# FFN norm factor on the products' results, a first pair of inner tiles without block sums, and weights transferred ahead of operands

## The chip, the cores and the metric

The kernel runs on one core of a Trainium2 chip. The metric is device time in microseconds (us) of one execution; lower is better. TensorE (PE in the profile) multiplies, VectorE (DVE), ScalarE (ACT) and GpSimd (POOL) work elementwise, and SyncE (SP) issues the transfers between the chip's memory (DRAM) and the on-chip buffers. Results of matmuls stand in eight banks of PSUM.

## What is computed

One step of a decoder layer for 1024 prompt tokens and eight decode tokens, all in float32; the kernel treats the 1032 tokens together. Cut to what the change touches:

```python
def rmsnorm(x, g):
    xf = x.astype(jnp.float32)
    y = xf * lax.rsqrt(jnp.mean(xf * xf, axis=-1, keepdims=True) + EPS)
    return (y * g.astype(jnp.float32)).astype(x.dtype)

def swiglu_half(x, g, w_gate, w_up, w_down):
    u = rmsnorm(x, g)
    return x + 0.5 * ((jax.nn.silu(u @ w_gate) * (u @ w_up)) @ w_down)

def hybrid_layer(x, p_emb, pos, lp, attend, retain):
    h = swiglu_half(x, lp['ffn1_norm'], lp['ffn1_w_gate'], lp['ffn1_w_up'], lp['ffn1_w_down'])
    u = rmsnorm(h, lp['mix_norm'])
    z = u @ lp['w_in']
    ...
    merged = (jax.nn.sigmoid(ga) * (o_att @ lp['w_branch_att'])
              + jax.nn.sigmoid(gr) * (o_ret @ lp['w_branch_ret']))
    h = h + merged @ lp['w_out']
    h = swiglu_half(h, lp['ffn2_norm'], lp['ffn2_w_gate'], lp['ffn2_w_up'], lp['ffn2_w_down'])
    gate = jax.nn.sigmoid(rmsnorm(h, lp['ple_norm']) @ lp['w_ple_gate'])
    ...
```

D_MODEL is 1024 and D_FF 2816. The norm's factor, the rsqrt of the mean square, is one number per token; the gain `g` is one number per feature.

## The kernel before

**Layout.** Features lie on the 128 partitions, tokens on the free axis: a token tile `ht` has 8 row tiles (`k`) of 128 features. The 1032 tokens are two halves (`tp` 0 and 1) of two columns each (`lr`), HC = 258 tokens a column. Every operand of a product is split into a high and a low part (`split`: ACT's cast at L103, then DVE's subtraction at L104), and each product is three matmuls, high·high, high·low, low·high.

**FFN, gate and up** (`Block.run`). The 22 inner tiles of 128 are taken in 11 pairs. For one pair, `unit` forms the 2×2 block product (two inner tiles by two halves of the features, against two halves of the features by two columns) from seven block products instead of eight: 7 × 4 × 3 = 84 matmuls per token half, at L323, L325 and L326. That needs sums of weight blocks (`Stream.early` and `Stream.make`, L264, L265, L281, L285) and sums of token blocks. The latter are made once per FFN by the generator `tokens(tp)`: squares (L437, L438), the norm factor `r` by Newton steps (`rstd2`, L340 to L359), `ht` times gain times `r` (`normed`, L456), sums (L465 to L480), and the splits into the seven blocks `b`. Both FFNs begin with units of pair 0 for `tp` 0 alone, while `tokens(1)` runs beside them; pair 0 for `tp` 1 is done at the end, between the two halves of pair 10. Results go through `gate` (ACT's Silu) and `up` into `s`, and from there to DRAM as `mid_d`.

**FFN, down** (`product`, L369 to L371). All 22 `m` tiles of a token half are loaded back (`fetch`, L600), and for each half `tp` and each half `o` of the features 22 weights are run into eight banks, 24 matmuls a weight. `Rows` transfers the weights (`wd`, L306), with three loads ahead. The evacuation at L618 is one operation a bank: 0.5 times the bank plus `h`.

**w_out** is the same `product`, with four banks, 64 weights of 256 columns and 12 matmuls a weight. Its operands `wm` are the merged branches that the stage before has stored to `mg_d` (L1310) and that are loaded at L1323, eight for each token half; `ht` is loaded at L1325. Evacuation (L1338), squares and, for `tp` 0, the token blocks of FFN 2 run beside it.

**What sets the order.** The program is written through a framework that orders the instructions of each engine by itself from the dependences and the pools' free buffers; each engine then runs its list in order. SP issues all of the transfers above in one list, so a transfer that waits holds up those behind it.

Of the kernel before, what the change touches and what calls it, by code (L numbers as in the profile page):

```python
# [10 lines left out]
F32 = mybir.dt.float32  # L11
# [9 lines left out]
P = 128  # L21
D = 1024
# [34 lines left out]
def body(ctx, tc, a):  # L57
# [240 lines left out]
    class Rows(Stream):  # L298


        def make(self, units):
            raws = []
            for i in range(len(units) + 3):
                if i < len(units):
                    t = self.rawp.tile([P, 512], F32, tag="q", name="wd")[:, :units[i].shape[-1]]
                    sp.dma_start(t, units[i])  # L306
                    raws.append(t)
                if i >= 3:
                    yield self.split(raws[i - 3])
# [66 lines left out]
    class Next:  # L376
# [5 lines left out]
        def open(self, prepare):  # L382
# [3 lines left out]
            self.first = prepare(self.ring)  # L386
# [23 lines left out]
    class Block:  # L410
# [5 lines left out]
        def open(self):  # L416
            self.w_st, self.right = ExitStack(), ExitStack()
            self.x0_st = ExitStack()
            pre = self.pre
            self.wp = self.w_st.enter_context(pools(pre + "w", 6))  # L420
            self.rawp = self.w_st.enter_context(pools(pre + "q", 8))
            bp = self.right.enter_context(pools(pre + "b0", side="right"))
            self.x1 = self.right.enter_context(pools(pre + "x1", side="right"))
            x0 = self.x0_st.enter_context(pools(pre + "x0", side="right"))
            self.bs = [bp.tile([P, 4, 7, 2, HC], F32R, name="b0"), None]
            self.hts = [x.tile([P, KT, 2 * HC], F32, name="ht") for x in (x0, self.x1)]

        def accs(self):
            return [self.x1.tile([P, HC], F32, tag=f"acc{i}", name="acc") for i in range(2)]

        def sq(self, accs, k, hv):
            for i in range(2):
                if k == 0:
                    act.activation(accs[i], hv[:, HV[i]], AF.Square)
                else:
                    t = self.x1.tile([P, HC], F32, tag="sq", name="sq", bufs=4)
# [3 lines left out]
        def tokens(self, tp, accs=None):  # L440

            ht, gi = self.hts[tp], self.gi
            if accs is None:
                accs = self.accs()
                for k in range(KT):
                    self.sq(accs, k, ht[:, k])
                    if k % 2:
                        yield
            r = [self.x1.tile([P, HC], F32, tag=f"r{i}", name="r") for i in range(2)]
            yield from rstd2(accs, D, r)  # L450
            bt = self.bs[tp]
            b11, b12, b21, b22 = (ht[:, 4 * i:4 * i + 4, HV[lr]] for i in range(2) for lr in range(2))

            def normed(t, half, lr):
                for k in range(4):
                    dve.scalar_tensor_tensor(t[:, k], t[:, k], gain(gi, 4 * half + k), r[lr], op0=ALU.mult, op1=ALU.mult)  # L456

            def splits(q, t):
                split(bt[:, :, q, 0], bt[:, :, q, 1], t)

            normed(b11, 0, 0)
            splits(0, b11)
            yield
            normed(b12, 0, 1)
            dve.tensor_tensor(b11, b12, b11, op=ALU.subtract)  # L465
            splits(1, b11)
            yield
            normed(b22, 1, 1)
            dve.tensor_tensor(b11, b22, b11, op=ALU.subtract)
            splits(2, b11)  # L470
            yield
            normed(b21, 1, 0)
            splits(3, b21)
            yield
            dve.tensor_tensor(b12, b22, b12, op=ALU.subtract)
            splits(4, b12)
            yield
            splits(6, b22)
            yield
            dve.tensor_tensor(b11, b21, b11, op=ALU.subtract)  # L480
            splits(5, b11)
            yield

        def stream(self):
# [4 lines left out]
        def run(self, builds, nxt, nxt_st, prepare):  # L489

            pre, bs, NP = self.pre, self.bs, NF // 2
            e_st = ExitStack()
            e = e_st.enter_context(pools(pre + "e", 18))
            stream = self.weights
# [1066 lines left out]
```

## Time and profile before

| quantity | value |
| --- | --- |
| runs, us | 2611.8, 2610.56, 2608.18 (median 2610.56) |
| profiled execution: its own time, its span | 2606.3 us, 2604.5 us |
| TensorE busy | 2455.9 us, 94% of the span |
| VectorE, ScalarE, GpSimd busy | 55%, 37%, 7% |
| mean granted clock of TensorE | 0.974 |
| moved | 355.24 MB, 136 GB/s over the span |

A group's row has line, engine, operation, output <- inputs, shapes and count, then busy us and the mean ns of one, then the idle time of the engine just before them and what ended it. A row of waits has engine, tile and line, what it waited for, and us in total, times, longest. A row of windows has busy us and instruction count of each engine, the granted clock of TensorE as a share of full speed, the busy share of the transfer engines, and GB/s.

### The profile page before, as it was taken

The numbers are of one execution on the slowest core, as the hardware profiler recorded it, in microseconds if no ns is written. First come the engines' busy times: TensorE is split into PE (matmuls) and PEld (weight loads), VectorE is DVE, ScalarE is ACT, GpSimd is POOL, SyncE is SP. The second block draws the span as 40 slices with busy tenths as digits, with TensorE's granted clock in tenths as the row PEclk, the third lists the DMA queues.
The fourth block names the chain that finished last, engine by engine and source line by source line (L and its number), as shares of the span: only waits on it lengthen the run. The fifth ranks groups of instructions, "written<-read, shape, count | busy, mean of one in ns | idle before, by whom it ended". The sixth has DMA issues, their size and how long they took to land.

```text
span 2604.5 us, 48647 instructions
## 1 busy us (share of the span) xinstructions
PE 2455.9 (94%) x19036; PEld 2364.9 (91%) x19036; DVE 1435.4 (55%) x3271; ACT 962.4 (37%) x2125; POOL 175.5 (7%) x220
## 2 busy tenths in 40 slices
PE   5999999899999999999999974979999998999998
PEld 5899999899999999999976664979999998999997
DVE  8765657733333656422577763696656676332345
ACT  5444445523222112211255531454444454222221
POOL 0000000001011101100142100000000000010111
PEclk9899999899999999999999987999999998999999
DMA  3223323869422122222034369333323248684311
GB/s 131 98 82 121 120 85 128 299 255 327 150 100 73 62 68 72 88 75 89 31 102 125 100 198 325 119 104 110 119 86 115 99 144 326 241 308 134 128 52 66
DMA packets 177031, 355.24 MB, mean 136 GB/s; under 512 B 19433, under 2 KB 68738, under 8 KB 176802
## 3 DMA queue, kind: packets, MB, share of 16 engines
q1 hardware_dynamic: 171682, 338.54, 37.8%
q0 software_dynamic: 5120, 13.59, 1.5%
q8 instruction: 150, 2.46, 0.4%
q14 instruction: 79, 0.65, 0.1%
HBM read 259.21 MB, written 91.80 MB: 135 GB/s over the span
## 4 chain that ended last, share of the span: by engine, by line
PE 87%; DVE 6%; DMA 4%; ACT 1%; issue 1%; POOL 0%; SPq 0%; DVEq 0%; POOLq 0%; ACTq 0%
PE ps L325 11%; PE ps L323 11%; PE ps L326 11%; PE ps L369 8%; PE ps L371 7%; PE ps L370 7%; PE ps L138 7%; PE ps L139 7%; PE ps L140 7%; PE ps L1074 2%; PE ps L1110 1%; PE ps L1099 1%; DVE w L104 1%; DMA wm<-mg_d 1%; DVE b L104 1%
## 5 line engine op out<-in xcount | busy, mean ns | idle before, releaser
L323 PE MATMUL ps<-b,w 128*128 128x258 f32 x2464 | 703.6, 286 | 10.9 <-ACT b L103 9.5
L325 PE MATMUL ps<-b,w 128*128 128x258 f32 x2464 | 706.9, 287 | 5.0 <-DVE b L104 5.0
L326 PE MATMUL ps<-b,w 128*128 128x258 f32 x2464 | 697.1, 283 | 12.3 <-DVE w L104 12.3
L326 PEld LDWEIGHTS ps<-b,w 128*128 128x128 f32 x2464 | 474.6, 193 | 12.9 <-DVE w L104 12.9
L323 PEld LDWEIGHTS ps<-b,w 128*128 128x128 f32 x2464 | 468.8, 190 | 13.7 <-ACT b L103 11.3
L325 PEld LDWEIGHTS ps<-b,w 128*128 128x128 f32 x2464 | 472.4, 192 | 6.6 <-DVE b L104 6.6
L369 PE MATMUL ps<-m,w 128*128 128x258 f32 x1408 | 401.8, 285 | 23.8 <-DMA m<-mid_d 23.8
L370 PE MATMUL ps<-m,w 128*128 128x258 f32 x1408 | 399.2, 284 | 0.0
L371 PE MATMUL ps<-m,w 128*128 128x258 f32 x1408 | 398.5, 283 | 0.0
L104 DVE TENSOR_TENSOR w<-wd,w 128x512 fp32r<-128x512 f32 (+1 forms) x240 | 152.8, 646 | 372.1 <-ACT w L103 347.7
L138 PE MATMUL ps<-u,w 128*128 128x344 f32 (+4 forms) x960 | 312.0, 326 | 3.8 <-DVE sz L147 3.8
L104 DVE TENSOR_TENSOR w<-wq,w 128x512 fp32r<-128x512 f32 x312 | 213.7, 688 | 180.5 <-ACT w L103 178.3
L139 PE MATMUL ps<-u,w 128*128 128x344 f32 (+4 forms) x960 | 308.5, 321 | 0.0
L140 PE MATMUL ps<-u,w 128*128 128x344 f32 (+4 forms) x960 | 307.9, 321 | 0.0
L369 PEld LDWEIGHTS ps<-m,w 128*128 128x128 f32 x1408 | 267.9, 190 | 24.2 <-DMA m<-mid_d 24.2
L103 ACT CAST w<-wd 128x512 fp32r<-128x512 f32 (+1 forms) x240 | 134.5, 561 | 416.1 <-PE ps L371 307.2
L370 PEld LDWEIGHTS ps<-m,w 128*128 128x128 f32 x1408 | 269.2, 191 | 0.0
L371 PEld LDWEIGHTS ps<-m,w 128*128 128x128 f32 x1408 | 268.0, 191 | 0.0
L103 ACT CAST w<-wq 128x512 fp32r<-128x512 f32 x312 | 191.9, 621 | 58.0 <-PE ps L326 34.2
L138 PEld LDWEIGHTS ps<-u,w 128*128 128x128 f32 (+1 forms) x960 | 180.5, 188 | 6.2 <-DVE sz L147 3.8
L139 PEld LDWEIGHTS ps<-u,w 128*128 128x128 f32 (+1 forms) x960 | 180.0, 187 | 0.9 <-issue 0.4
L140 PEld LDWEIGHTS ps<-u,w 128*128 128x128 f32 (+1 forms) x960 | 180.1, 188 | 0.6
(297 smaller groups left out, 3706.3 us busy)
## 6 DMA issues: line engine op xcount, KB each, us to landing
mid_d<-s SPq DMA_DIRECT2D x88, 516.0 KB, 3.7
m<-mid_d SPq DMA_DIRECT2D x88, 516.0 KB, 6.0
wd<-in_f1down_dram SPq DMA_DIRECT2D x88, 256.0 KB, 3.7
wd<-in_f2down_dram SPq DMA_DIRECT2D x88, 256.0 KB, 4.1
ct<-in_cache_dram SPq DMA_DIRECT2D x128, 128.0 KB, 2.1
wq<-in_f1gate_dram SPq DMA_DIRECT2D x52, 256.0 KB, 4.1
wq<-in_f1up_dram SPq DMA_DIRECT2D x52, 256.0 KB, 2.6
wq<-in_f2gate_dram SPq DMA_DIRECT2D x52, 256.0 KB, 4.1
```

Of the source, the lines that this page charges most:

```text
L103: act.copy(dst_hi, src)
L104: dve.tensor_tensor(dst_lo, src, dst_hi.bitcast(F32), op=ALU.subtract)
L138: pe.matmul(ps, w[:, 0, ws], x[:, 0, xs], start=start, stop=False)
L139: pe.matmul(ps, w[:, 0, ws], x[:, 1, xs], start=False, stop=False)
L140: pe.matmul(ps, w[:, 1, ws], x[:, 0, xs], start=False, stop=stop)
L323: pe.matmul(ps, w[:, 0, js], t[:, 0], start=q in (0, 1, 3) and j == 0, stop=False, skip_group_check=True)
L325: pe.matmul(ps, w[:, 0, js], t[:, 1], start=False, stop=False, skip_group_check=True)
L326: pe.matmul(ps, w[:, 1, js], t[:, 0], start=False, stop=j == kh - 1, skip_group_check=True)
L369: pe.matmul(ps, w[:, 0, ws], t[:, 0, HV[n % 2]], start=f == 0, stop=False)
L370: pe.matmul(ps, w[:, 0, ws], t[:, 1, HV[n % 2]], start=False, stop=False)
L371: pe.matmul(ps, w[:, 1, ws], t[:, 0, HV[n % 2]], start=False, stop=f == nf - 1)
L1074: pe.matmul(ps[:, :w], qc[hd][:, i * P:(i + 1) * P], kc[hd][:, j:j + w], start=True, stop=not diag)
```

## The change

- The norm factor leaves the token blocks. `plain_tokens` scales `ht` by the gain alone (DVE for `tp` 0, ACT for `tp` 1); `r` is kept in a pool of its own and multiplied into the gate results before Silu, and, with the 0.5, into the down results. The up results are not scaled.
- The first pair of inner tiles is done with eight block products (`plain`), on blocks that need no sums, for (tile, half) (0,0), (1,0), (1,1), (0,1), with 12 weights from `Rows`. `sums` and `last_sum` make the other blocks meanwhile. An FFN then has 384 matmuls in place of 336 for this pair, and `stream` starts with pair 1. At the end pair 10 is done for `tp` 0, then for `tp` 1.
- `Rows` issues its first three transfers when it is made, which in `w_out` and in the down product is ahead of the operands. In `w_out` only the operands of `tp` 0 are fetched first; those of `tp` 1 after the first product; `ht` after five `wm`.
- Ring loads for the stage after an FFN are issued behind the last `m` load. `mst` has four buffers instead of two. The raw weights' pool is closed after the gate and up units and opened again with five buffers.

```diff
     class Rows(Stream):
+        def __init__(self, wp, rawp, units, ahead):
+            super().__init__(wp, rawp, units, ahead)
+            self.units, self.raws = iter(units), []
+            for _ in range(3):
+                self.fetch()
...
+        def plain_tokens(self, tp, k0=0, k1=KT):
+
+            ht = self.hts[tp]
+            b11, b12, b21, b22 = self.blocks(tp)
+            for i, (qs, ts) in enumerate((((0, 1), (b11, b12)), ((3, 6), (b21, b22)))):
+                for k in range(4 * i, 4 * i + 4):
+                    if tp == 0:
+                        dve.tensor_scalar(ht[:, k], ht[:, k], gain(self.gi, k), None, op0=ALU.mult)
+                    else:
+                        act.activation(ht[:, k], ht[:, k], AF.Copy, scale=gain(self.gi, k))
+                    yield
+                for q, t in zip(qs, ts):
+                    self.splits(tp, q, t)
+                    yield
...
-            self.weights = Stream(self.wp, self.rawp, [u_ for p_ in pair for u_ in p_] + pair[0] + pair[-1], 0)
+            self.weights = Stream(self.wp, self.rawp, [u_ for p_ in pair[1:] for u_ in p_] + pair[-1], 2)
...
+            def plain(ws, tp, lr):
+                ps = allbank()
+                for h_ in range(2):
+                    for j in range(4):
+                        js, t = slice(j * P, j * P + P), bs[tp][:, j, (0, 1, 3, 6)[2 * h_ + lr]]
+                        pe.matmul(ps[:, :HC], ws[h_][:, 0, js], t[:, 0], start=h_ + j == 0, stop=False)
+                        pe.matmul(ps[:, :HC], ws[h_][:, 0, js], t[:, 1], start=False, stop=False)
+                        pe.matmul(ps[:, :HC], ws[h_][:, 1, js], t[:, 0], start=False, stop=h_ + j == 4)
+                return ps
...
+            for n, (l, tp) in enumerate(((0, 0), (1, 0), (1, 1), (0, 1))):
+                if n != 2:
+                    ws = [rows.take() for _ in range(4)]
+                pg = [plain(ws[:2], tp, lr) for lr in range(2)]
+                if n in (0, 2) and accs[tp] is not None:
+                    for _ in self.norm(tp, accs[tp]):
+                        pass
+                pu = [plain(ws[2:], tp, lr) for lr in range(2)]
+                ts = []
+                for lr in range(2):
+                    t = pt()
+                    ts.append(t)
+                    dve.tensor_tensor(t, pg[lr][:, :HC], self.r[tp][:, HV[lr]], op=ALU.mult)
+                    act.activation(t, t, AF.Silu)
...
             def gate(q, tp, ps):
...
-                elif q == 5:
+                    return
+                r = self.r[tp][:, HV[q in (4, 6)]]
+                if q == 5:
                     gated[tp, q] = t = et()
-                    act.activation(t, ps, AF.Silu)
+                    dve.tensor_tensor(t, ps, r, op=ALU.mult)
+                    defer(1, act.activation, t, t, AF.Silu)
                 else:
                     gated[tp, q] = t = kept[tp, {3: 0, 4: 1, 6: 2}[q]]
                     dve.tensor_tensor(t, t, ps, op=ALU.add)
-                    defer(1, act.activation, t, t, AF.Silu)
+                    defer(1, silu, t, r)
...
-            for i, tp in ((NP - 1, 0), (0, 1), (NP - 1, 1)):
+            for tp in TPS:
                 unit(stream, b, 4, (tp,), gate, tick)
-                unit(stream, b, 4, (tp,), up(i, sgp), tick)
+                unit(stream, b, 4, (tp,), up(NP - 1), tick)
...
+                        if tp == 1 and o == 0:
+                            with tc.issue_after(self.loaded.ins):
+                                nxt.first = prepare(nxt.ring)
...
-                            dve.scalar_tensor_tensor(hv, banks[n][:, :HC], 0.5, hv, op0=ALU.mult, op1=ALU.add)
+                            t = tmp.tile([P, HC], F32, tag="c", name="c")
+                            dve.scalar_tensor_tensor(t, banks[n][:, :HC], 0.5, self.r[tp][:, HV[n % 2]],
+                                                     op0=ALU.mult, op1=ALU.mult)
+                            dve.tensor_tensor(hv, hv, t, op=ALU.add)
...
-                st = mt.tile([P, 2, 2 * HC], F32R, tag="mst", name="mst")
+                st = mt.tile([P, 2, 2 * HC], F32R, tag="mst", name="mst", bufs=4)
...
-        for tp in TPS:
+
+        def fetch(tp):
             for f in range(KT):
                 xs[tp, f] = t = wm.tile([P, 2, 2 * HC], F32R, tag="wm", name="wm")
                 sp.dma_start(t.bitcast(F32), mg_d[f, tp])
-            for k in range(0, KT, 4):
-                sp.dma_start(two.hts[tp][:, k:k + 4], hs_d[:, k:k + 4, both(tp)])
...
+                if f == KT // 2:
+                    for k in range(0, KT, 4):
+                        sp.dma_start(two.hts[tp][:, k:k + 4], hs_d[:, k:k + 4, both(tp)])
+
+        fetch(0)
...
+                if tp == 0 and o == 0:
+                    fetch(1)
...
-                steps = two.tokens(0, accs)
+                steps = chain(two.norm(0, sums_of[0]), two.plain_tokens(0), two.sums(0))
```

How the lists move is seen at three places. First VectorE at the start of FFN 1, from the last squares to the first token blocks (`acc`: sums of squares, `sv`, `sz`, `st`: Newton steps of the norm, `w`: low halves of weights, `b_97`, `b_105`: low halves of token blocks). Before:

```order
L438 TENSOR_TENSOR acc<-acc,sq 128x258 x4
L456 SCALAR_TENSOR_TENSOR ht<-ht,gains,r 128x258 x4
L104 TENSOR_TENSOR w<-wq,w 128x512
L456 SCALAR_TENSOR_TENSOR ht<-ht,gains,r 128x258
L264 TENSOR_TENSOR ws<-wq 128x512
L104 TENSOR_TENSOR b_97<-ht,b_97 128x4x258
L265 TENSOR_TENSOR wq<-wq 128x512
```

And in the changed kernel:

```order
L472 TENSOR_SCALAR ht<-ht,gains 128x516
L104 TENSOR_TENSOR b_105<-ht,b_105 128x4x258
L453 TENSOR_TENSOR acc<-acc,sq 128x258
L104 TENSOR_TENSOR b_105<-ht,b_105 128x4x258
L472 TENSOR_SCALAR ht<-ht,gains 128x516 x3
L350 TENSOR_SCALAR sv<-ps_276 128x6
L453 TENSOR_TENSOR acc<-acc,sq 128x258
```

The first two low halves of token blocks now stand ahead of the norm's Newton steps (`sv` on), where before the first stood behind all of them and behind the scaling at L456.

Second, SP between the last gate and up results of FFN 1 and its down product; in brackets is what an issue waits for (DMAHW: an earlier transfer of SP, by its slot; the other names are engines). Before:

```order
L533 DMA mid_d<-s 128x1032 [waits DMAHW0_49,DVE_49]
L533 DMA mid_d<-s 128x1032 [waits DMAHW1_49,DVE_49]
L608 DMA h<-in_xT_dram 128x4x516 [waits DMAHW2_49]
L600 DMA m<-mid_d 128x1032 [waits DMAHW3_49,DMAHW1_49]
L600 DMA m<-mid_d 128x1032 [waits DMAHW4_49]
```

And in the changed kernel:

```order
L514 DMA mid_d<-s 128x1032 [waits DVE_49] x2
L673 DMA h<-in_xT_dram 128x4x516
L665 DMA m<-mid_d 128x1032 [waits DMAHW4_49]
L665 DMA m<-mid_d 128x1032 [waits DMAHW5_49]
L665 DMA m<-mid_d 128x1032 [waits DMAHW6_49]
```

The first `m` waited for the slot of the last `mid_d` store too (DMAHW1), and now waits for one older transfer only.

Third, SP from the last stores of the merged branches to the weights of `w_out`. Before:

```order
L1310 DMA mg_d<-mst 128x1032
L1325 DMA ht<-hs_d 128x4x516
L1310 DMA mg_d<-mst 128x1032 x2
L1325 DMA ht<-hs_d 128x4x516
L1323 DMA wm<-mg_d 128x1032 x16
L306 DMA wd<-in_wout_dram 128x256 x20
```

And in the changed kernel, where four more `wm` rows stand some 40 issues earlier, among the gate loads of the stage before:

```order
L1383 DMA mg_d<-mst 128x1032 x3
L1397 DMA wm<-mg_d 128x1032 x2
L311 DMA wd<-in_wout_dram 128x256 x3
L1400 DMA ht<-hs_d 128x4x516 x2
L1397 DMA wm<-mg_d 128x1032 x2
L311 DMA wd<-in_wout_dram 128x256 x11
L1397 DMA wm<-mg_d 128x1032 x5
L1400 DMA ht<-hs_d 128x4x516 x2
L1397 DMA wm<-mg_d 128x1032 x3
```

All of `wm` and `ht` stood ahead of the first weight; now two `wm` do, and the second half's operands follow the fourteenth weight.

More of the change, by code (lines that the diff above doesn't have):

```diff
@@ L298, in body, with fetch @@
     class Rows(Stream):
-        def make(self, units):
[L302 to L309, printed above, removed]
+        def __init__(self, wp, rawp, units, ahead):
[3 more added lines that the diff above has]
+                self.fetch()
+        def fetch(self):
+            src = next(self.units, None)
+            if src is not None:
+                t = self.rawp.tile([P, 512], F32, tag="q", name="wd")[:, :src.shape[-1]]
+                sp.dma_start(t, src)
+                self.raws.append(t)
+        def make(self, units):
+            for _ in units:
+                self.fetch()
+                yield self.split(self.raws.pop(0))
     xbank, ybank, zbank = rotation(0, 4), rotation(4, 2), rotation(6, 2)
@@ L435, in sq @@
                 else:
-                    t = self.x1.tile([P, HC], F32, tag="sq", name="sq", bufs=4)
+                    t = self.x1.tile([P, HC], F32, tag="sq", name="sq", bufs=3)
                     act.activation(t, hv[:, HV[i]], AF.Square)
                     dve.tensor_tensor(accs[i], accs[i], t, op=ALU.add)
[L440 to L450, printed above, removed]
-            bt = self.bs[tp]
[L452 to L464, printed above, removed]
-            dve.tensor_tensor(b11, b12, b11, op=ALU.subtract)
[L466 to L473, printed above, removed]
@@ new lines, in norm, with blocks, splits @@
+        def norm(self, tp, accs):
+            return rstd2(accs, D, [self.r[tp][:, HV[lr]] for lr in range(2)])
+        def blocks(self, tp):
+            return [self.hts[tp][:, 4 * i:4 * i + 4, HV[lr]] for i in range(2) for lr in range(2)]
+        def splits(self, tp, q, t):
+            bt = self.bs[tp]
+            split(bt[:, :, q, 0], bt[:, :, q, 1], t)
+        def plain_tokens(self, tp, k0=0, k1=KT):
[11 more added lines that the diff above has]
+                    yield
@@ L474, in tokens, with sums @@
+        def sums(self, tp):
+            b11, b12, b21, b22 = self.blocks(tp)
+            dve.tensor_tensor(b11, b12, b11, op=ALU.subtract)
             yield
             dve.tensor_tensor(b12, b22, b12, op=ALU.subtract)
-            splits(4, b12)
+            self.splits(tp, 4, b12)
             yield
-            splits(6, b22)
+            dve.tensor_tensor(b22, b22, b11, op=ALU.subtract)
+            self.splits(tp, 2, b22)
             yield
-            dve.tensor_tensor(b11, b21, b11, op=ALU.subtract)
@@ L492, in run @@
             e_st = ExitStack()
             e = e_st.enter_context(pools(pre + "e", 18))
-            stream = self.weights
+            stream = self.stream()
             now, due = [0], {}
@@ L525, in gate, with up @@
                     dve.tensor_tensor(t, t, ps, op=ALU.add)
[L526 to L533 removed]
+                    defer(1, silu, t, r)
+            def up(i):
                 def evac(q, tp, ps):
@@ L599, in fetch @@
                 mids[tp, f] = t = mp.tile([P, 2, 2 * HC], F32R, tag="m", name="m")
-                sp.dma_start(t.bitcast(F32), self.mid_d[f, tp])
+                self.loaded = sp.dma_start(t.bitcast(F32), self.mid_d[f, tp])
             for f in range(NF):
@@ L633, in run @@
                             nxt.squares(tmp, tp, 4 * o + k, ht[:, k])
+            self.q_st.close()
             self.w_st.close()
@@ L639, in body @@
     one.open()
-    one.stream().ahead = 1
     for tp in TPS:
@@ L645, in body @@
     mix = Next(ring_st, "r", 1, u1_d)
-    one.run([one.tokens(tp) for tp in TPS], mix, u_st, lambda ring: [ring.load("rv", i) for i in range(2)])
+    one.run(mix, u_st, lambda ring: [ring.load("rv", i) for i in range(2)])
     ring, u, r, wv0 = mix.ring, mix.u, mix.r, mix.first
@@ L1291, in fetch @@
                 gates[tp, o, lr].append(t)
+        for i in range(2):
+            wa[i] = ring.load("batt", i)
         for at in todo[:5]:
@@ L1350, in body @@
     last = Next(ctx, "s", 3, u2_d)
-    two.run([None, two.tokens(1, accs)], last, ctx, lambda ring: [ring.load("plg", o) for o in range(2)])
+    last = Next(ctx, "s", 3, u2_d)
+    two.run(last, ctx, lambda ring: [ring.load("plg", o) for o in range(2)], [None, sums_of[1]])
     ring, u, r, plw = last.ring, last.u, last.r, last.first
```

121 lines of the change are left out of this document (74 added, 47 removed).

## The prediction

> **What bounds the kernel now.** I read the page first: the busy shares, the chain that ended last, the costliest groups.
>
> ```profile
> span 2604.5 us, 48647 instructions
> PE 2455.9 (94%) x19036; PEld 2364.9 (91%) x19036; DVE 1435.4 (55%) x3271; ACT 962.4 (37%) x2125; POOL 175.5 (7%) x220
> PE 87%; DVE 6%; DMA 4%; ACT 1%; issue 1%; POOL 0%; SPq 0%; DVEq 0%; POOLq 0%; ACTq 0%
> L323 PE MATMUL ps<-b,w 128*128 128x258 f32 x2464 | 703.6, 286 | 10.9 <-ACT b L103 9.5
> L326 PE MATMUL ps<-b,w 128*128 128x258 f32 x2464 | 697.1, 283 | 12.3 <-DVE w L104 12.3
> L369 PE MATMUL ps<-m,w 128*128 128x258 f32 x1408 | 401.8, 285 | 23.8 <-DMA m<-mid_d 23.8
> ```
>
> TensorE bounds: 87% of the chain, and only 2604.5 − 2455.9 = 148.6 us in which it has no matmul. So a gain can come only from that idle time, from matmuls run at the slow clock, or from fewer matmuls, and the change adds matmuls. Next, windows, to learn the pace and to see where PE falls short of it.
>
> ```profile
> 200.00:400.00 200.00, 200.00 (x1663) 200.00 (x1662) 121.40 (x247) 91.80 (x208) 0.00 (x0) 1.00 0.29 102
> 25.00:45.00 20.00, 12.90 (x56) 11.50 (x57) 18.27 (x28) 11.01 (x16) 0.00 (x0) 1.00 0.12 40
> 0.00:95.00 95.00, 36.93 (x112) 25.17 (x113) 0.93 0.32 113
> 1700.00:1777.00 77.00, 32.51 (x111) 22.25 (x111) 0.93 0.34 114
> ```
>
> Columns: length, busy time (count) of PE, weight loads, VectorE (DVE), ScalarE (ACT), GpSimd, clock, DMA share, GB/s; the last two rows hold line L323 alone, so PE and weight loads only. The pace is 200/1663 = 0.1203 us a matmul. In 25:45 there are 56, where 166 would fit, and DVE is busy for 18.27 of 20 us. L323 is a third of an FFN's gate/up matmuls: 3 × 112 = 336, one pair of inner tiles for both token halves, is done at 95 us in FFN 1, and 3 × 111 = 333 at 1777 (336 at 1777.5) in FFN 2. I compare the changed kernel at these two points, since what follows them is dense in both.
>
> **First pair of FFN 1.** Waits and matmul starts in 0:120, and VectorE's groups up to 92 us:
>
> ```profile
> PE ps L340 <- DVE acc L438: 11.5, 1, 11.5
> PE ps L323 <- ACT b L103: 9.5, 7, 3.9
> PE ps L325 <- DVE b L104: 5.0, 6, 1.3
> 25.26 0.42 PE L326 MATMUL ps<-b,w 128*128 128x258 f32 x1
> ...
> 27.20 0.42 PE L326 MATMUL ps<-b,w 128*128 128x258 f32 x1
> L104 DVE TENSOR_TENSOR b<-ht,b 128x1032 fp32r<-128x1032 f32 x14 | 16.9, 1230 | 0.7 <-ACT b L103 0.7
> L456 DVE SCALAR_TENSOR_TENSOR ht<-ht,gains,r 128x258 f32<-128x258 f32 x32 | 13.7, 481 | 0.7 <-ACT r L351 0.7
> L104 DVE TENSOR_TENSOR w<-wq,w 128x512 fp32r<-128x512 f32 x19 | 12.7, 683 | 1.5 <-ACT w L103 1.5
> 21.99 0.69 DVE L104 TENSOR_TENSOR w<-wq,w 128x512 fp32r<-128x512 f32 x1 [0.73 <-ACT w L103]
> L1093 DVE TENSOR_SCALAR pr<-pr,rs 128x640 f32<-128x640 f32 x8 | 4.4, 548 | 0.1
> ```
>
> PE starves on token blocks `b`: each needs the norm factor, four L456 and a 1.23 us low half. Between bursts it idles, and inside one the matmuls stand (27.20 − 25.26)/9 = 0.215 us apart (nine steps, unbroken), the slow pace, though the clock of 25:45 reads 1.00. The change takes the factor out of this path: gains only (a 128x516 tensor_scalar, estimated just under the 548 ns of the 640-wide row), and the plain pair reads four blocks that are slices of the scaled tokens, so no sums come first. Blocks and first weights are then ready at about 20.7 us (first low weight at 21.99 before; the squares no longer stand ahead of all of it). The pair takes 384 matmuls instead of 336. From 20.7: 384 × 0.1203 = 46.2, about 2 for the norm's rank-one matmuls, 2.4 for a cold start (priced below), makes 71.3. VectorE has to keep up: 16 block halves × 1.23 = 19.7, 8 sums of the same size 9.8, 17 weight operations of 512 columns × 0.68 = 11.6, 28 accumulations and 24 evacuations of 258 columns × 0.36 = 18.7 (pace from the evacuation row below), 8 scalings × 0.5 = 4, Newton steps about 4: 67.8 us from 5.7 on, so until 73.5. That is a tie with PE; I add 3 and put the end at 74.3. Gain 95 − 74.3 = 20.7, taken as 21. Bounds: 25 if VectorE never delays PE, 10 if each of some ten hand-overs costs the mean L323 wait of 9.5/7.
>
> **w_out and the first pair of FFN 2.** Waits of PE in 1585:1760, SP's issues, and VectorE in w_out:
>
> ```profile
> PE ps L369 <- ACT w L103: 33.0, 2, 32.7
> PE ps L326 <- DVE w L104: 10.0, 2, 9.7
> PE ps L371 <- DVE w L104: 4.4, 4, 1.9
> 1588.39 0.63 SPq L1325 DMA_DIRECT2D ht<-hs_d  x1
> 1589.12 17.68 SPq L1323 DMA_DIRECT2D wm<-mg_d  x16
> 1607.82 12.45 SPq L306 DMA_DIRECT2D wd<-in_wout_dram  x13
> 1590.00:1620.00 30.00, 2.39 (x11) 2.39 (x12) 2.22 (x6) 2.19 (x6) 0.00 (x0) 0.50 0.96 366
> 510.00:515.00 5.00, 3.51 (x16) 3.51 (x17) 0.00 (x0) 0.00 (x0) 0.00 (x0) 0.50 1.00 398
> 515.00:520.00 5.00, 5.00 (x37) 5.00 (x36) 0.69 (x1) 0.68 (x2) 0.00 (x0) 0.81 1.03 420
> L104 DVE TENSOR_TENSOR w<-wd,w 128x256 fp32r<-128x256 f32 x17 | 6.4, 417 | 1.8 <-ACT w L103 1.8
> ```
>
> The largest single wait, 32.7 us, names ScalarE, but it is a weight: the first `wd` is issued at 1607.82 behind 16 `wm` of 0.53 MB and an `ht`, at 366 GB/s. In the new order four `wm` are loaded during the stage before (in place of two `ht`), and only two `wm` and the weights themselves lie between the last store, about 1588.4, and the third weight: 1.06 + 0.39 MB at 366 GB/s is 4 us, 2 to land and cast, so PE restarts at 1595. A cold start: 16 + 37 matmuls in the 8.5 us after 511.5, where 53 × 0.1203 = 6.4 would do, so 2.1, say 2.4 to be safe. The queue then bites back twice. The fourth weight is behind `ht` x2 and `wm` x2, 3.2 MB or 8.6 us, against three cold weights' work of 12 × 3 × 0.215 = 7.7: 1 us. The fifteenth is behind the second half's eight `wm` and two `ht`, 6.3 MB or 17 us, against the six or seven weights then buffered, 12 × 0.1203 = 1.44 each: 7.5 us and a second cold start, 10 in all. w_out has 64 weights × 12 = 768 matmuls: 1595 + 92.4 + 2.4 + 1 + 10 = 1700.8. In the second half VectorE makes 32 halves of weights (417 ns), one set of plain blocks and its sums, about 40 us in 46, so the first FFN units find blocks ready and the 9.7 and the 4.4 us waits go. 384 matmuls (46.2) and 2 for the norm: 1749, with 2.5 of slack 1751.5. Gain 1777.5 − 1751.5 = 26. Bounds: 36 without the queue's stall, 11 if it is twice that and VectorE is 5 late.
>
> **Up to down, in each FFN.** The chain at 501 us and PE's two waits:
>
> ```profile
> 501.45 4.12 DMA mid_d<-s
> 505.58 5.86 DMA m<-mid_d
> PE ps L369 <- DMA m<-mid_d: 11.8, 1, 11.8
> PE ps L369 <- DMA m<-mid_d: 12.0, 1, 12.0
> ```
>
> Here `m` of tile 0 waits for the last store's landing (4.12), and then lands in 5.86 behind an `h` load. In the new order the first four `m` wait only for a queue slot, so they follow at once; store and `h` still pass first, about 2.1 MB. Four ring loads of 0.5 MB that ran there move into the down product. I take 3.5 each, 7 together; bounds 3 (stores late by the last pair) and 12 (the whole 4.12 and the rings' share).
>
> **What it costs.** Evacuating the down banks:
>
> ```profile
> 575.10 2.92 DVE L618 SCALAR_TENSOR_TENSOR h<-ps,h 128x258 f32<-128x258 f32 x8 [1.94 <-PE ps L371]
> PE ps L665 <- DMA u<-u_d: 3.4, 1, 3.4
> PE ps L349 <- DVE sz L147: 2.5, 1, 2.5
> ```
>
> Eight banks in 2.92 us, 0.36 each, are now two operations each, 5.9 us. Between products the banks come free every 0.74 us, while the next product needs one every 3 × 0.1203 = 0.36; but the first evacuation can start 2.5 us before the product ends, so of 8 × 0.74 = 5.9 about 0.3 shows: six such boundaries, 2 (0 to 6). At a block's end 3 us join the norm chain behind the last bank, of which the two waits above are part; `u` loads now stand behind one store instead of three and more matmuls cover the Newton steps: 1.5 per block, 3 (0 to 8). In the units of the last pair, one token half each, VectorE does nearly 20 us in 20.2 us of PE: 1 (0 to 5). In ten pairs per FFN, eight more multiplications per gate unit: 8 × 0.36 = 2.9 us in 40.4 us of PE, on top of 121.40/200 = 61%, so 68%: nothing on the path, since PE is busy through all of 200:400 beside it; if that cover were gone it would be 20 × 2.9 = 58. The third `batt`'s place in the queue is the same; two more `mst` buffers are part of the 26. Pair 0 is no longer taken up again for the second half at the end of an FFN: its matmuls are in the 384, and the 16 raw weights of its two visits become 12, which only eases the queue. The 96 added matmuls (11.5 us) are in both ends above already. Costs 6 (0 to 19).
>
> **Sum.** 21 + 26 + 7 − 6 = 48 off the profiled execution's 2606.3: 2558.3. The median of the runs is 2610.56, 4.3 more; I predict 2562.6, so 2563. All terms at their low ends give 10 + 11 + 3 − 19 = 5, at their high ends 25 + 36 + 12 = 73.
>
> **Rivals.** First, weights still behind operands: the first `ht` of w_out, and the fourth weight behind it, wait for the last three stores to land; if that takes 4 us longer under a full queue, and only two weights are buffered at the second half's loads, the stalls are 4 + (17 − 2 × 1.44 − 7.5) = 10.6 more: 2574. For it: a DMA share of 0.96 in 1590:1620. Against: two `wm` and three weights are issued ahead of that wait.
> Second, the plain pair runs in bursts: if VectorE hands blocks over one at a time, as in 25:45, PE never gets to the fast pace in the first pair: 384 × (0.215 − 0.1203) = 36 more, 2599. For it: the tie at 73.5. Against: four blocks serve 384 matmuls, where seven served 336. The Trainium skill, TensorE: Matmul & The Clock Gate, Part 1: The HAM clock gate, says that the full clock comes only after about 3.4 us of sustained work and goes after an idle window as long. By that rule this rival needs pauses of the longest kind, 3.9 us here, and with the mean one, 9.5/7 = 1.4, the clock would rise and only the pauses be lost, some 10 us: 2573. The trace does not decide between the two: it has the long pause and the slow pace at one place.
> Third, the other side: VectorE becomes the bound in gate units, because the new multiplication stands between the bank's release and the next weight's low half. At the full 2.9 us for each of 20 gate units it costs 58 and turns the result to 2621; it decides from 48/20 = 2.4 us a unit. For it: q = 5's bank is now freed by VectorE, not ScalarE. Against: 39% of VectorE is idle there.
> Fourth, nothing: the stalls come back elsewhere, 2610.
>
> **Chances.** Forecast 0.64, first rival 0.16, second 0.10, third 0.05, fourth 0.03, better than the high bounds 0.02. Faster by over 0.2% (5 us, about what can be told from no change): 0.64 + 0.16 + 0.10 + 0.02 = 0.92; within 0.03; slower 0.05. The range goes from 2538 (the high ends) to 2592, past the first rival and short of the second.
>
> **What would show it.** Right: PE dense from 21 us, 384 plain matmuls done near 74; PE back at 1595, a wait of some 7 us for a weight near 1620; the two `m` waits at 8 to 9 us; VectorE near 68% in 200:400 with no PE wait. Wrong: PE waits on `b` in 25:70, on VectorE inside gate units, or a weight wait over 15 us in w_out.

## The result and the profile after

The changed kernel takes 2572.03 us (median of three runs, 2569.03 to 2574.33), against 2610.56 before: a ratio of 0.9853 with a 95% interval of 0.9831 to 0.9875, 38.5 us faster. Run again beside the last experiments, it was 0.9845 (0.9829 to 0.9862). The forecast was 2563, 47.6 faster.

The page of the changed kernel, with the lines that answer to those of before:

```profile
span 2566.1 us, 48859 instructions
PE 2454.5 (96%) x19132; PEld 2365.7 (92%) x19132; DVE 1472.4 (57%) x3379; ACT 957.7 (37%) x2089; POOL 180.0 (7%) x220
PE 87%; DMA 5%; DVE 4%; issue 1%; ACT 1%; SPq 1%; POOL 0%; POOLq 0%; DVEq 0%; ACTq 0%
L333 PE MATMUL ps<-b,w 128*128 128x258 f32 x2240 | 636.7, 284 | 0.0
L377 PE MATMUL ps<-m,w 128*128 128x258 f32 x1408 | 402.6, 286 | 30.1 <-DMA m<-mid_d 26.3
```

96 more matmuls, and TensorE is busy for 1.4 us less: the slow pace of the first pairs is all but gone. Idle time fell from 148.6 to 111.6 us. The gate and up units (L333; L325 before) wait for nothing any more; the down product (L377; L369 before) waits more, not less.

What PE waited for, over the whole span of the changed kernel (engine, tile and line, waited for; us in total, times, longest):

```profile
PE ps L377 <- DMA m<-mid_d: 26.3, 2, 13.3
PE ps L377 <- ACT w L103: 20.5, 5, 9.8
PE ps L348 <- DVE acc L453: 13.0, 2, 12.6
PE ps L540 <- ACT w L103: 3.5, 1, 3.5
```

The 32.7 us ahead of w_out are down to 9.8, plus smaller ones; the two waits for the first `m` are 26.3 where they were 23.8.

The two first pairs, by the first and last start of one of the three lines of the plain product (a line's summary, in 0:200 and in 1560:1750), and the last start of the gate and up units (L334, in 300:600):

```profile
L540 PE MATMUL ps<-b,w x128: 277/283/583, 19.4 to 71.3; 128*128 128x258 f32 x128
L540 PE MATMUL ps<-b,w x128: 277/283/365, 1686.0 to 1734.7; 128*128 128x258 f32 x128
L334 PE MATMUL ps<-b,w x488: 276/281/287, 300.0 to 475.7; 128*128 128x258 f32 x163
```

Such first and last starts cut the span into stretches; before, the same points are 95, 1777.5 and, for the last gate and up matmul, 499.4. The sum of the stretches is the whole difference:

| stretch, us | before | after | gain | forecast |
| --- | --- | --- | --- | --- |
| start to the end of FFN 1's first pair | 95.0 | 71.3 | 23.7 | 21 |
| pairs 1 to 10, both FFNs | 404.4, 405.2 | 404.4, 404.4 | 0.8 | −1 |
| last gate and up matmul to first down matmul | 12.1, 12.3 | 13.6, 13.3 | −2.5 | 7 |
| down product, both FFNs | 255.9, 255.6 | 258.7, 259.6 | −6.8 | −2 |
| last down matmul to the next stage's projection | 42.0, 5.5 | 40.7, 5.3 | 1.5 | −3 |
| projection to the end of the branch stage | 775.0 | 776.9 | −1.9 | 0 |
| from there to the end of FFN 2's first pair | 193.1 | 169.1 | 24.0 | 26 |
| last stretch | 148.4 | 148.8 | −0.4 | 0 |

That is 38.4, the difference of the two spans. The two large gains came out within 3 us each. The whole miss is 9.6, about what the third row missed alone, where 7 were to be won and 2.5 were lost. That the rest cancels is luck: the down products lost 4.8 more than forecast, and the row behind them lost 4.5 less.

One caution on all that follows. Executions of one kernel differ by up to 13 us. The two profiled executions of the changed kernel are 10.3 us apart, and 6.6 of that lies between the projection and the end of the branch stage, which no experiment touches. In one of them (the repeat, first two rows) TensorE's granted clock was 0.50 there from a pause of 1.2 us on, at 1324.5, until 1338.2, and stayed there while TensorE was busy again; in the other (last two rows, the same place) it stayed at 1.00 through the same pause.

```profile
1325.65 0.37 PE L1247 MATMUL ps<-ident,ckvs 128*8 128x128 f32 x1 [1.18 <-DVE nm L1152]
1327.00:1335.00 8.00, 8.00 (x42) 4.55 (x40) 2.88 (x11) 1.89 (x6) 0.58 (x1) 0.50 0.41 115
1322.55 0.27 PE L1247 MATMUL ps<-ident,ckvs 128*8 128x128 f32 x1 [1.27 <-DVE nm L1152]
1324.00:1332.00 8.00, 7.83 (x57) 4.51 (x56) 6.18 (x23) 4.06 (x14) 2.04 (x2) 1.00 0.44 131
```

So parts are judged below by their stretches in the trace, and medians stand beside them.

### The profile page after: what moved, and what is told of

It is laid out like the page before. It is cut to its first block, busy times and chain, and to the rows that moved or that the text cites. A ratio compares the mean times of both kernels' runs of the same rounds, so it can differ in the third digit from the quotient of the medians.

```text
span 2566.1 us, 48859 instructions
## 1 busy us (share of the span) xinstructions
PE 2454.5 (96%) x19132; PEld 2365.7 (92%) x19132; DVE 1472.4 (57%) x3379; ACT 957.7 (37%) x2089; POOL 180.0 (7%) x220
## 3 DMA queue, kind: packets, MB, share of 16 engines
q1 hardware_dynamic: 170530, 336.44, 38.4%
## 4 chain that ended last, share of the span: by engine, by line
PE 87%; DMA 5%; DVE 4%; issue 1%; ACT 1%; SPq 1%; POOL 0%; POOLq 0%; DVEq 0%; ACTq 0%
PE ps L333 11%; PE ps L331 10%; PE ps L334 10%; PE ps L138 7%; PE ps L139 7%; PE ps L140 7%; PE ps L377 7%; PE ps L379 6%; PE ps L378 6%; PE ps L1145 2%; DMA m<-mid_d 2%; PE ps L1181 1%; PE ps L1170 1%; PE ps L540 1%; PE ps L541 1%; PE ps L542 1%
## 5 line engine op out<-in xcount | busy, mean ns | idle before, releaser
L333 PE MATMUL ps<-b,w 128*128 128x258 f32 x2240 | 636.7, 284 | 0.0
L331 PE MATMUL ps<-b,w 128*128 128x258 f32 x2240 | 632.9, 283 | 0.0
L334 PE MATMUL ps<-b,w 128*128 128x258 f32 x2240 | 630.2, 281 | 0.0
L377 PE MATMUL ps<-m,w 128*128 128x258 f32 x1408 | 402.6, 286 | 30.1 <-DMA m<-mid_d 26.3
L334 PEld LDWEIGHTS ps<-b,w 128*128 128x128 f32 x2240 | 427.0, 191 | 0.0
L333 PEld LDWEIGHTS ps<-b,w 128*128 128x128 f32 x2240 | 424.8, 190 | 0.0
L331 PEld LDWEIGHTS ps<-b,w 128*128 128x128 f32 x2240 | 421.4, 188 | 0.1
L104 DVE TENSOR_TENSOR w<-wd,w 128x512 fp32r<-128x512 f32 (+1 forms) x264 | 164.9, 641 | 314.2 <-ACT w L103 311.9
L377 PEld LDWEIGHTS ps<-m,w 128*128 128x128 f32 x1408 | 267.8, 190 | 32.5 <-issue 26.7
L103 ACT CAST w<-wd 128x512 fp32r<-128x512 f32 (+1 forms) x264 | 148.3, 567 | 385.5 <-PE ps L379 225.4
L104 DVE TENSOR_TENSOR w<-wq,w 128x512 fp32r<-128x512 f32 x264 | 181.4, 688 | 148.4 <-ACT w L103 146.0
L103 ACT CAST w<-wq 128x512 fp32r<-128x512 f32 x264 | 163.5, 620 | 33.0 <-PE ps L334 23.6
```

What stands on the lines that cost most here:

```text
L103: act.copy(dst_hi, src)
L104: dve.tensor_tensor(dst_lo, src, dst_hi.bitcast(F32), op=ALU.subtract)
L331: pe.matmul(ps, w[:, 0, js], t[:, 0], start=q in (0, 1, 3) and j == 0, stop=False, skip_group_check=True)
L333: pe.matmul(ps, w[:, 0, js], t[:, 1], start=False, stop=False, skip_group_check=True)
L334: pe.matmul(ps, w[:, 1, js], t[:, 0], start=False, stop=j == kh - 1, skip_group_check=True)
L377: pe.matmul(ps, w[:, 0, ws], t[:, 0, HV[n % 2]], start=f == 0, stop=False)
```

## The experiments

Theory W is the prediction's: the first `m` was late because its issue waited for the last store to land. Theory Q is the rival formed from the traces: the transfers ahead of it in SP's one queue set its time. The issues of the changed kernel at the end of FFN 1 (start, length, issues; each of the two last rows is a window that begins later, so the count is what was left):

```profile
477.62 0.90 SPq L514 DMA_DIRECT2D mid_d<-s  x2
478.56 1.10 SPq L673 DMA_DIRECT2D h<-in_xT_dram  x1
479.71 26.93 SPq L665 DMA_DIRECT2D m<-mid_d  x22
487.89 18.75 SPq L665 DMA_DIRECT2D m<-mid_d  x15
489.17 17.47 SPq L665 DMA_DIRECT2D m<-mid_d  x14
```

Eight issues are in flight here: the eighth `m`, at 487.89, waits for the slot of `h`, eight issues earlier, and the ninth, 1.28 us later, for that of the first `m`, which PE used at 489.29. So the first `m` was issued nearly at once behind the stores, as the prediction said (479.71, and 505.58 − 501.45 = 4.1 after the last store's issue before), and then lay 9.5 us in the queue behind 2.1 MB, where it had been 5.9.

**h behind m.**

```diff
-                        sp.dma_start(ht, self.src[:, 4 * o:4 * o + 4, both(tp)])
+                        with tc.issue_after(self.loaded.ins):
+                            sp.dma_start(ht, self.src[:, 4 * o:4 * o + 4, both(tp)])
```

> Changed kernel, but in each FFN the h load of the first down product is issued behind the last m load instead of ahead of the first; two weight loads move up into its place. Theory Q (the first m is late because the stores and h lie ahead of it in one queue): in the trace of the changed kernel h is issued at 478.56 and its slot comes free at 487.89, the first m lands 1.3 us behind it, so without h the wait of 13.3 us falls by 3 to 4 us in each FFN, 6 to 8 us in all, to about 2565. Theory W (only the wait for the last store's landing mattered, as predicted): nothing changes, 2572.

Measured 2561.69 us, 0.9834 (0.9811 to 0.9857) of before. The wait fell from 13.3 and 13.0 to 11.1 and 10.9:

```profile
PE ps L377 <- DMA m<-mid_d: 22.1, 2, 11.1
```

That is 4.3 in all, less than the 6 to 8 expected; two weight loads of 0.26 MB went ahead of the first `m` in h's place and held SP for 2.3 us. The down products are 3.7 us shorter as well (257.6 and 257.0): with two more weights ahead, PE waits for none there, as it does in the changed kernel for the tenth. The rest of the difference in the medians lies within the scatter. W expected nothing.

**The wait put back.** The units of the last pair run in the order second half, first half, and the tile stored last is loaded and used first, so its load waits for that store.

```diff
-            for tp in TPS:
+            for tp in (1, 0):
                 unit(stream, b, 4, (tp,), gate, tick)
...
-            for f in range(NF):
+            FS = [NF - 1] + list(range(NF - 1))
+            for f in FS:
                 fetch(0, f)
...
```

> Changed kernel, but the first m that is loaded is the one stored last (the last inner tile of the first token half, whose units now run last), so it waits for the last store to land, as in the kernel before; the down products take the tiles in that order. Theory W: the wait of 13.3 us grows by the store's landing less what the queue hides, 3.5 us in each FFN, 7 in all, 2579. Theory Q: the queue moves stores and h in that time anyway, at most 1 us in each FFN, 2572 to 2574.

Measured 2570.52 us, 0.9862 (0.9845 to 0.9879), and the waits as without it:

```profile
PE ps L377 <- DMA m<-mid_d: 25.6, 2, 12.9
```

W falls: a wait for the landing that the prediction priced at 3.5 us costs nothing, since store and `h` fill the queue for that time anyway.

**Ring loads early.** The loads for the next stage issued where the kernel before has them.

```diff
             nxt.open()
+            nxt.first = prepare(nxt.ring)
...
-                        if tp == 1 and o == 0:
-                            with tc.issue_after(self.loaded.ins):
-                                nxt.first = prepare(nxt.ring)
```

> Changed kernel with the ring loads of the following stage issued where the kernel before has them, among the last gate and up units, instead of behind the last m. As predicted (they take a share of the rate ahead of the first m): the waits of 13.3 and 13.0 us grow by 1 to 2 each, 2574 to 2576. Rival (they end before the last stores begin): unchanged, 2572.

Measured 2598.75 us, 0.9958 (0.9945 to 0.9971): 29.4 us more than the changed kernel on the same chip, and neither theory had said so. The waits for `m` are as they were (26.1, against 26.3); those for weights, 20.5 us over the whole span of the changed kernel, are 44.1:

```profile
PE ps L377 <- ACT w L103: 44.1, 5, 12.3
PE ps L377 <- DMA m<-mid_d: 26.1, 2, 13.3
...
472.80 2.33 SPq L311 DMA_DIRECT2D wd<-in_f1down_dram  x5
475.24 0.36 SPq L113 DMA_DIRECT2D raw<-in_rk_dram  x1
...
482.03 27.07 SPq L666 DMA_DIRECT2D m<-mid_d  x22
```

With the rings in between only five down weights go out ahead of the 22 `m` (nine in the changed kernel), the sixth is behind all of them, and the down products take 272 us. So the rings' move did not speed up the first `m`; it keeps the weights ahead of the operands. Whether only five go out because their pool now has five buffers, or because the rings hold up SP's list (the first of the five goes out at 472.80 here, at 466.99 in the changed kernel), was not tried.

**w_out's weights behind its operands.**

```diff
+        with tc.issue_after(last_in.ins):
+            rows = Rows(two.wp, two.rawp, [a["wout"][f][:, o * 256:o * 256 + 256]
+                                           for tp in TPS for o in range(4) for f in range(KT)], 3)
...
```

> Changed kernel, but in w_out all wm and ht of both token halves are issued ahead of the first weight, as in the kernel before (four wm still go out during the stage before). As predicted: 12 wm and four ht, 10.5 MB at 366 GB/s, make one wait of about 30 us, in place of three of 9.8, 2.7 and 6.1 with two more cold starts of 2: 8 to 10 us longer, 2580 to 2582. Rival (the front of w_out is bound by its bytes, and their order does not matter): the same, 2572 to 2574.

Measured 2581.19 us, 0.9904 (0.9879 to 0.9929). From the end of the branch stage to the end of w_out it takes 130.5 us, in the changed kernel 120.0, and before 136.2. The waits in 1540:1760:

```profile
PE ps L377 <- ACT w L103: 33.2, 1, 33.2
```

The order of weights and operands is worth 10.5 us, as expected; bytes alone do not bind.

**The second half's operands spread.** In place of one block behind the fourteenth weight, they go one by one between the weights of the second to the fourth product.

```diff
-                if tp == 0 and o == 0:
-                    fetch(1)
...
+                    if tp == 0 and o in (1, 2) and f % 2:
+                        with tc.issue_after(rows.last.ins):
+                            fetch(1, 4 * (o - 1) + f // 2)
...
```

> Changed kernel, but in w_out the second half's eight wm are issued one at a time between weights of the second and third product and its ht at the fourth, instead of in one block behind the fourteenth weight. Theory: the wait of 6.1 us at 1609 is the fifteenth weight behind that block; it goes, with the cold start behind it (2 us): 8 us, 2564. Rival (bytes bind): the wait comes back at the start of the second half or in pieces, 2570 to 2574.

Measured 2558.78 us, 0.9807 (0.979 to 0.9824). The same stretch takes 109.8 us instead of 120.0, 10.2 less; of the 18.6 us that PE waits there in the changed kernel remain:

```profile
PE ps L377 <- ACT w L103: 12.0, 2, 9.8
```

The 6.1 us wait and its cold start are gone and do not come back, so the prediction's "queue bites back" was rightly placed; the block cost 10 us, as priced.

**The factor back in the token blocks.** The plain pair stays; the blocks are scaled by gain and factor behind the norm, and the later multiplications go.

```diff
-                        dve.tensor_scalar(ht[:, k], ht[:, k], gain(self.gi, k), None, op0=ALU.mult)
...
+                        dve.scalar_tensor_tensor(ht[:, k, HV[lr]], ht[:, k, HV[lr]], gain(self.gi, k),
+                                                 self.r[tp][:, HV[lr]], op0=ALU.mult, op1=ALU.mult)
...
```

> Changed kernel with the norm factor back in the token blocks (scaling by gain and factor in columns of 258, behind the norm), hence no multiplication on gate results and one operation a bank in down; plain first pair and transfers as changed. As predicted (the factor on the path to the blocks holds up FFN 1's start): the plain pair ends at about 80 instead of 71.3, FFN 2 0 to 3 later, down 1 earlier in each FFN: 2578. Rival (the plain pair alone gives the start's gain, the norm is hidden beside loads): the pair ends by 73, and without the extra operations the total is the same or lower, 2568 to 2572.

Measured 2573.16 us, 0.9881 (0.9866 to 0.9896). The first line of its plain product, and what PE waits for there:

```profile
L541 PE MATMUL ps<-b,w x128: 278/283/584, 24.1 to 81.8; 128*128 128x258 f32 x128
PE ps L541 <- ACT b L103: 3.4, 1, 3.4
```

The plain pair begins 4.7 us later (24.1, against 19.4) and ends at 81.8 instead of 71.3: of FFN 1's 23.7 us the factor's move gives about 10.5, and plain blocks with the rest of the change about 13. The 10.5 is not the path alone: this run also scales in twice as many operations, all of them on VectorE, and PE waits 3.6 us for a weight's low half of VectorE within the pair. No run separates the two. In FFN 2 the pair takes the same 49 us, because its first blocks are made beside w_out. Part of the 10.5 goes back in the down products, 257.6 and 256.5 us here.

**No multiplication on gate results.** Part of the norm is left out of the result.

```diff
             def silu(t, r):
-                dve.tensor_tensor(t, t, r, op=ALU.mult)
                 act.activation(t, t, AF.Silu)
...
```

> Changed kernel without the multiplication of the norm factor on the gate results of pairs 1 to 10, so that part of the norm is left out of the result. As predicted (hidden beside PE): the stretch from the end of the plain pair to the end of gate and up stays at 404 us in each FFN, 2572. Rival (VectorE on the path in gate units): it shortens by 1 us or more a unit, 20 in all, 2552.

Measured 2566.21 us, 0.9852 (0.9836 to 0.9867), on a chip where the kernel before has 2603.50; the changed kernel's own ratio is the same. The stretch is 476.0 − 71.6 = 404.4, to the tenth as in the changed kernel:

```profile
L540 PE MATMUL ps<-b,w x128: 277/283/584, 19.2 to 71.6; 128*128 128x258 f32 x128
L334 PE MATMUL ps<-b,w x489: 276/281/287, 300.0 to 476.0; 128*128 128x258 f32 x163
```

VectorE's extra work in the gate units is fully hidden; the third rival is out. (VectorE is busy for 137.99 of the 200 us in 200:400 of the changed kernel, 69% where 68% was forecast, and PE for all 200.)

**One operation a bank in down.** The norm factor is left out of the down results.

```diff
-                            dve.scalar_tensor_tensor(t, banks[n][:, :HC], 0.5, self.r[tp][:, HV[n % 2]],
-                                                     op0=ALU.mult, op1=ALU.mult)
-                            dve.tensor_tensor(hv, hv, t, op=ALU.add)
+                            dve.scalar_tensor_tensor(hv, banks[n][:, :HC], 0.5, hv, op0=ALU.mult, op1=ALU.add)
```

> Changed kernel with the down evacuation back at one operation a bank, so that the norm factor is left out of the down results. As predicted (boundaries 1 and block ends 1.5 in each FFN): 5 us in all, 2567, the down products of 258.7 and 259.6 us about 257.5. Rival (the evacuation explains all of what the down products grew by): both fall to 256, 7 us in all, 2565.

Measured 2563.03 us, 0.9843 (0.9828 to 0.9858). The down products (first and last start of L377 here, then in the changed kernel) take 256.6 and 256.2 us, instead of 258.7 and 259.6:

```profile
L377 PE MATMUL ps<-m,w x704: 277/283/554, 489.3 to 748.0; 128*128 128x258 f32 x176
L377 PE MATMUL ps<-m,w x704: 276/283/554, 488.8 to 745.4; 128*128 128x258 f32 x176
```

They are 5.5 us shorter, but not all of that is the second operation. Summed over the steps from one matmul start to the next, what exceeds the pace of 0.12 at the three boundaries between the products of an FFN is 0.3, 1.2 and 0.35 us in the changed kernel, 3.7 over both FFNs, and nothing in this run or in the kernel before. The other 3.1 of the 6.8 us that the down products grew by is a wait for the tenth weight, which stands behind all 22 `m`; it scatters, and is 2.6 in this run and 8.2 in the repeat of the changed kernel. At the blocks' ends nothing shows. Nor does a gain show in the whole time: 0.9843 of the kernel before on this chip, where the changed kernel has 0.9853 and 0.9845, with an interval of 4 us on either side.

**The parts together.** h behind the last `m`, later weights behind the third `m`, spread operands in w_out, and an evacuation in groups of four.

```diff
-                            dve.tensor_tensor(hv, hv, t, op=ALU.add)
+                            cs.append(t)
+                            if n % 4 == 3:
+                                for i in range(n - 3, n + 1):
+                                    hv = ht[:, i // 2, HV[i % 2]]
+                                    dve.tensor_tensor(hv, hv, cs[i], op=ALU.add)
...
```

> Changed kernel with what the first four runs point to, together: h behind the last m load, the tenth and later down weights behind the third m (so that the first m follows the last store directly), the second half's wm and ht of w_out between weights, and the down evacuation in groups of four (four products with the factor, which free four banks, then four additions, with four buffers). If the parts add: the waits for the first m fall from 13.3 and 13.0 to about 9.5 each (7 in all), w_out is 10 shorter, the evacuation gives 1 in each FFN: 19 less, 2553. Rival (the same transfer time comes back in each place): only w_out's 10, 2562.

Measured 2551.76 us, 0.9803 (0.979 to 0.9817), the span 2550.0. The waits for `m` fell as expected, but the down products grew to 261 us, and the trace of the first says why (waits in 484.9:746.5):

```profile
PE ps L383 <- DMA m<-mid_d: 9.2, 1, 9.2
PE ps L383 <- ACT w L103: 3.1, 1, 3.1
```

The tenth weight stood behind 22 `m` and `h`, as it does behind 22 `m` in the changed kernel. At the three boundaries between products PE now loses nothing; since the runs with only `h` moved or only the operands spread still lose their 1.9 us in each FFN there, that is the evacuation in fours. With ten `m` up front and the rest in turn with weights:

```diff
+                def more(f):
+                    if f + AH < NF:
+                        with tc.issue_after(rows.last.ins):
+                            fetch(0, f + AH)
...
```

> The combination again, with the second fault taken out that its trace shows: there the tenth down weight stood behind all 22 m and h and made PE wait 3.1 and 3.5 us. Now ten m and h go first, then one weight and one m in turn. If that fault is all: the down products fall from 261 to about 257.5 us each, 7 less than the first combination's 2550.0 in the span, 2543. Rival (m then comes too late, or h does): no gain, 2550.

Measured 2545.59 us (2545.27 to 2546.52), 0.9753 (0.9737 to 0.9769). Its waits in the whole span, and a down product of 255.2 us:

```profile
PE ps L383 <- DMA m<-mid_d: 18.4, 2, 9.4
PE ps L383 <- ACT w L103: 13.1, 2, 10.5
L383 PE MATMUL ps<-m,w x704: 277/283/554, 485.8 to 741.0; 128*128 128x258 f32 x176
```

**The changed kernel again**, on the same chip:

> The changed kernel as it is, again, on the chip of the combination. Both theories: 0.985 of the kernel before.

Measured 2569.39 us, 0.9845 (0.9829 to 0.9862). The combination is 23.8 us faster than it. Against the first trace of the changed kernel the stretches give 25.0: 7.9 from the last gate and up matmul to the first down matmul, 7.5 in the down products, 9.6 from the branch stage to the end of FFN 2's first pair. It is the fastest version found, 63 us below the kernel before.

## Why the prediction was right, and where it was off

**The start of FFN 1** was 21 and is 23.7. The estimate of a plain pair from 20.7 to 74.3 is 19.4 to 71.3 in the trace; the 3 us of slack for the tie between PE and VectorE were not needed, and the second rival (bursts) did not come: PE waited 3.5 us ahead of the pair and not once within it. (The 1.00 that the clock of 25:45 read in the prediction is no measurement: that trace's clock record begins at 42.4 us, and up to there the matmuls stand 0.215 us apart, behind it 0.12.) That taking the norm out of the path lets the pair begin and end earlier is shown by the run with the factor in the blocks: 24.1 to 81.8 with the norm back in it.

**w_out and FFN 2's first pair** were 26 and are 24.0. PE was back 9.8 us after the last branch matmul (10 forecast), the fourth weight cost 2.7 (1 forecast), the fifteenth 6.1 (7.5) and a cold start. The terms were sized by counting what stands ahead of each weight in the queue and dividing by the 366 GB/s of one window; that was enough. The measured 2572 lies nearer to the first rival's 2574 than to the forecast, but by chance: that rival wanted 10.6 us more of stalls in w_out, and they did not come.

**Up to down** is the step that failed, "I take 3.5 each, 7 together". The chain of waits of before named the store's landing (4.12) and then the load (5.86), and the prediction took the first as a price. It was also time in which the queue moved the stores and `h`. Take the wait away, and the load lies that much longer behind the same bytes: 9.5 instead of 5.9. The text named those 2.1 MB ahead of the first `m` and still took most of the 4.12. Its lower bound, 3, excluded a loss, and the term is −2.5. Most of the loss is that the stores themselves go out later. The last gate and up matmul starts at 499.4 and 2182.7 before, and at 475.7 and 2139.1 in the changed kernel; the stores behind it (two rows of before, then FFN 2 of the changed kernel, whose FFN 1 is shown above):

```profile
500.51 1.27 SPq L533 DMA_DIRECT2D mid_d<-s  x2
2183.86 1.26 SPq L533 DMA_DIRECT2D mid_d<-s  x2
2141.30 0.80 SPq L514 DMA_DIRECT2D mid_d<-s  x2
477.09 0.76 DVE L104 TENSOR_TENSOR s<-e,s 128x258 fp32r<-128x258 f32 x2
```

That is 1.1 us behind the last matmul in both FFNs before, and 1.9 and 2.2 after, 1.9 us in all. In the last row VectorE makes the last two low halves of `s` back to back; the text let late stores lower its gain to 3 and no further.

**Rings.** The prediction counted their removal as a small help to the first `m`. It gives none there; it buys 13 us in each FFN by getting nine down weights out ahead of the operands instead of five. The text had not seen this dependence, and why it is five stays open.

**Down.** Boundaries were 2 and are 3.7, and the block ends were 3 and are a gain of 1.5, no more than two traces of the changed kernel differ by (40.7 and 42.1 us to the projection in FFN 1). The mechanism of the boundaries stood in the text (a bank every 0.74 us against 0.36), the size did not. Its own numbers give more than the 0.3 a boundary that it took: the eighth bank's multiplication ends 7 × 0.74 + 0.36 − 2.5 = 3.0 us after the product, and the next product wants that bank after 7 × 0.36 = 2.5, so 0.5, or 3 for six. VectorE and PE at the first boundary of the changed kernel:

```profile
556.46 0.75 DVE L687 SCALAR_TENSOR_TENSOR c<-ps,r 128x258 f32<-128x258 f32 x2
557.13 1.31 DVE L689 TENSOR_TENSOR h<-h,c 128x258 f32<-128x258 f32 x2
558.37 0.75 DVE L687 SCALAR_TENSOR_TENSOR c<-ps,r 128x258 f32<-128x258 f32 x2
558.45 0.28 PE L379 MATMUL ps<-m,w 128*128 128x258 f32 x1
558.84 0.39 PE L377 MATMUL ps<-m,w 128*128 128x258 f32 x1
PE ps L377 <- ACT w L103: 1.6, 1, 1.6
```

Two additions take 1.31 us where the multiplications ahead of them took 0.75; the next multiplication starts behind them, at 558.37, and PE's next step is 0.39 instead of 0.12. Why the additions slow down was not tried. The last row is a wait in the down product of FFN 2 and belongs to the other 3.1 us of the growth: the tenth weight, behind all 22 `m`. The prediction has no term for it. In the second combination, with the evacuation in fours and `m` and weights in turn, both losses are gone, and the first down product takes 255.2 us.

**Gate units**: hidden, as forecast, to 0.1 us.

## What to carry to other kernels

A wait in the chain is worth what the queue does not do during it: before pricing the removal of a wait on a transfer, ask what the same queue moves in that time, and whether that must stand ahead at all. Moving a load that is needed late behind those needed first is the cheaper fix, but look at which buffers the loads behind it then hold. Work that hangs on a late per-token factor can start early if the factor is linear and goes on the product instead; its price shows where results leave PSUM, so free the banks first and do the second operation after.

## What was not expected of the hardware

Behind stores the transfers slow down for some us. In the changed kernel the first `m` lands 11.6 us after the first of the two `mid_d` stores is issued. The stores begin to move about 1.7 us after their issue, and then (windows as above; the last row is the second combination, without `h`):

```profile
480.00:482.00 2.00, 0.00 (x0) 0.00 (x0) 0.00 (x0) 0.00 (x0) 0.00 (x0) 0.73 0.99 398
482.00:484.00 2.00, 0.00 (x0) 0.00 (x0) 0.00 (x0) 0.00 (x0) 0.00 (x0) 0.50 0.87 237
486.00:488.00 2.00, 0.00 (x0) 0.00 (x0) 0.00 (x0) 0.00 (x0) 0.00 (x0) 0.50 1.05 426
482.00:484.00 2.00, 0.00 (x0) 0.00 (x0) 0.00 (x0) 0.00 (x0) 0.00 (x0) 0.50 0.98 312
```

The stores move at 398 GB/s, `h` behind them begins at 237, and the `m` that follow at 426. It is not the 2 KB rows of `h` alone: in 5:13 of the same trace rows of 2 KB move at 391 GB/s, and without `h` the rate behind the stores still falls to 312. What slows the first loads behind stores was not tried.

TensorE's granted clock can fall to 0.50 at a pause of 1.2 us and stay there for up to 14 us, though TensorE has work again after the pause, in one execution and not in the next. A fall began in this pause in four of the thirteen profiled executions. The cause stays open, and so does how much of the scatter between runs of one kernel it makes.
